# Residual stream of a two-layer trunk kept token-major: output projections with moving weights, norms along rows, modulation as rows

## The chip, the cores and the metric

The kernel runs on one core of a Trainium2 chip. The metric is the device time of one execution in microseconds (us). The engines are PE (TensorE, matrix products and transposes), DVE (VectorE), ACT (ScalarE), POOL (GpSimd) and SP (SyncE, which here issues most of the transfers). PE keeps 128 rows of a stationary matrix and streams columns of a moving one past it; results land in PSUM, which has banks of 512 fp32 columns by 128 partitions.

## The reference

640 tokens (128 of a prompt, 512 of a sample) of width D = 1024 go through two layers. The prompt and the sample have different modulation vectors, so each of the six modulation rows of a layer exists twice.

```python
for layer in range(DEPTH):
    mod = (silu(cond) @ w_mod[layer] + b_mod[layer])[:, None, :]
    sh1, sc1, g1, sh2, sc2, g2 = split(mod, 6, axis=-1)
    h = _modulate(x, norm_mix_g[layer], sh1, sc1)
    y, st = mixer(h, ...)          # layer 0: attention + gated delta, layer 1: SSD; ends in  o @ w_out
    x = x + g1 * y
    h = _modulate(x, norm_mlp_g[layer], sh2, sc2)
    x = x + g2 * _sq_relu_mlp(h, w_mlp_in[layer], w_mlp_out[layer])
return _rms_norm(x, final_norm_g)

def _modulate(x, gain, shift, scale):
    return _rms_norm(x, gain) * (1 + scale) + shift
def _sq_relu_mlp(h, w_in, w_out):
    a = maximum(h @ w_in, 0)
    return (a * a) @ w_out
```

In layer 1 the mixer's output is itself normed over 2048 features before w_out.

## The kernel before

**Layout.** The residual stream is feature-major: `xt` has 128 partitions of features, 8 blocks of features (KT), 640 tokens in the free dimension. All large products are made of three: each operand is split into a high part of a shorter type and a low part that is what is left, and hi x hi, lo x hi and hi x lo are added in PSUM. `wload` (L251) brings 1 MB of weights (`wraw`) by SP, `wpart` (L258) makes `whi` on ACT (L263) and `wlo` on DVE (L266).

**Products.** `gemm` (L273) makes one output tile: 128 output features (stationary weights) by 320 tokens (moving, half of the 640, HU), 8 blocks of features x 3 products = 24 products (`gps`, L287). `stage` (L291) goes over blocks of 256 output features, both halves of the tokens, two tiles each. For the second MLP product the 4096 hidden features come in four blocks b of 1024; `residual` (L513) adds each block's result, times the gate, to `xt` in one DVE operation per token class (L517).

**Norms.** The sum over features runs across partitions, so it is made on PE: `token_r` (L430) squares on ACT (L446), adds with a matrix of ones into four groups of 32 PSUM partitions (`stps`, L448), turns the sums into a column (`stc`, L456), takes the reciprocal root on DVE (L225 to L230), and spreads it over partitions again (`rbps`, L466). `pins` and `NPIN` hold these small products between fixed numbers of products of the last `gemm`s. `modulate` (L473) then makes `hh` and `hl`, the split input of the next stage, per block of features.

**Modulation.** `mod_steps` (L316) makes 512 of the 6144 outputs of `silu(cond) @ w_mod` per chunk c, in two half steps of 4 blocks k. Six chunks of layer 0 run in `delta_in`, between the inputs of the delta heads, with one small product per k, split into four of 128 columns that go to four groups of 32 PSUM partitions (L331). The other 14 chunks run in the first MLP with the sums over k on DVE (L352) and ACT and a short product at the end (`macc`, `msel`). `mod_out` (L306) turns the result into columns.

**Stages in time**: first norm and attention inputs (to 100 us), delta inputs with modulation (100 to 235), attention and delta heads (to 505), output projection `oute` with the norm ahead of the MLP (508 to 590), first MLP (to 1062, with the norm ahead of layer 1), SSD mixer (to 1553), output projection `outo` with its norm (to 1702), second MLP and `final` (L1584).

The order on each engine is set by a scheduler at build time from the order in the code and from when buffers come free; `issue_after` fixes single places.

Of the kernel before, what the change touches and what calls it, by code (L numbers as in the profile page):

```python
# [11 lines left out]
F32 = mybir.dt.float32  # L12
# [27 lines left out]

NPIN = (16, 8, 30, 24)
# [20 lines left out]
def _stream(i):  # L62
# [28 lines left out]
    for c in range(4):  # L91
        put(("oute", c), _cols(i["w_out_even"][0], c * 256, c * 256 + 256))
# [6 lines left out]
    for c in range(4):  # L99
        for kh in range(2):  # L100
            put(("outo", c, kh), _cols(i["w_out_odd"][0][kh * D:(kh + 1) * D], c * 256, c * 256 + 256))
    for layer in range(2):
        for b in range(4):
            for c in range(4):
                c0 = b * D + c * 256
                put(("m1", layer, b, c), _cols(i["w_mlp_in"][layer], c0, c0 + 256))
            for c in range(4):
                put(("m2", layer, b, c), _cols(i["w_mlp_out"][layer, b * D:(b + 1) * D], c * 256, c * 256 + 256))
# [3 lines left out]
def _params(i):  # L112
# [18 lines left out]
    put(("bmod", 1), _fm(i["b_mod"][1]))  # L131
    put(("gmix", 1), _fm(i["norm_mix_g"][1]))
    for layer in range(2):
        put(("gmlp", layer), _fm(i["norm_mlp_g"][layer]))
    put("gfin", _fm(i["final_norm_g"]))
# [57 lines left out]
class Prog:  # L193
    def __init__(self, nc, tc, ctx, io, widx, pidx, cidx, csmall, taps=None):
        self.nc, self.tc, self.ctx, self.io = nc, tc, ctx, io
        self.turn, self.share = 0, False
        self.sqb = 2
        self.behind = None
        self.mlast = None
        self.pins = []  # L200
        self.widx, self.pidx, self.cidx, self.csmall = widx, pidx, cidx, csmall
# [66 lines left out]

    def wblock(self, key, n=256):
        raw = self.wload(key, n)  # L270
        return [self.wpart(raw, c, min(P, n - c)) for c in range(0, n, P)]

    def gemm(self, w, xs, hf, half, m=P, cols=None):  # L273
# [6 lines left out]
        todo = [(k, q) for k in range(n) for q in range(3)]  # L280
        while todo:
            pin, m = self.pins.pop(0) if self.pins else (None, len(todo))
            if m > len(todo):
                self.pins.insert(0, (pin, m - len(todo)))
            with self.tc.issue_after(pin.ins) if pin else nullcontext():
                for k, q in todo[:m]:
                    self.nc.tensor.matmul(ps, ws[k // KT][q // 2][:, k % KT, :], xs[q % 2][k][:, c], start=k == 0 and q == 0, stop=k == n - 1 and q == 2)  # L287
            todo = todo[m:]
        return ps

    def stage(self, keys, xs, half, evac, tail=None, side=None):  # L291

        for i in range(0, len(keys), 2):
# [5 lines left out]
            for hf in range(2):  # L299
                for j, w in enumerate(tiles):  # L300
                    evac(2 * i + j, hf, self.gemm(w, xs, hf, half))
                if tail and i + 2 >= len(keys):
                    tail(hf)


    def mod_out(self, layer, m, ps):  # L306

        nc = self.nc
        n = ps.shape[1] // 32
        t = self.small.tile([P, P], F32, name="modt", tag="modt")[:, :32 * n]  # L310
        nc.vector.transpose(out=t, in_=ps)
        nc.vector.tensor_tensor(
            out=self.mod[layer][:, m:m + n, :], in0=t.rearrange("p (m c) -> p m c", c=32)[:, :, 0:2],
            in1=self.par(("bmod", layer))[:, m:m + n].rearrange("p (m o) -> p m o", o=1).to_broadcast([P, n, 2]), op=ALU.add)

    def mod_steps(self, todo, landing, pool=None, after=None):  # L316
# [11 lines left out]
        def product(lhs, x, start, stop):  # L328
            x = x.rearrange("p (m c) -> p m c", c=P)
            for q in range(4):  # L330
                nc.tensor.matmul(ps[32 * q:32 * q + 32], lhs, x[:, :, 32 * q:32 * q + 32], start=start, stop=stop)  # L331

        for i in range(n + 1):
            if i < n:
# [4 lines left out]
                raws.append(raw.rearrange("p (k c) -> p k c", c=512))  # L339
            if i:  # L340
                layer, c = todo[(i - 1) // 2]
                if i % 2:
                    ps = self.pmod.tile([P, 512], F32, name="modps", tag="mod")[:, :P]
# [1295 lines left out]
```

## Time and profile before

| | us |
|---|---|
| median of 3 runs | 2166.95 (2163.21 to 2169.73) |
| the profiled execution | 2170.79 |
| its span, first to last instruction | 2168.8 |
| PE busy | 2085.4 |
| DVE busy | 1353.2 |
| ACT busy | 908.3 |
| POOL busy | 158.5 |

The span is what the trace covers; the execution's own time is 2 us longer. Busy time is a sum over the whole span, so it says which engine is full on average, and not in which stage another one is waited for. Two products that follow each other overlap, so a product's duration is longer than its distance to the next; costs on PE are read from starts.

### The profile page before, as it was taken

Reading aid. Unit: us, or ns where it says so; the run is one execution under the profiler, and the core shown is the slowest. Engines: PE = TensorE matmul, PEld = TensorE weight load, DVE = VectorE, ACT = ScalarE, POOL = GpSimd, SP = SyncE. Lnnn points to the kernel's source line nnn. Section 1 sums busy time; section 2 is a strip of 40 time slices with the busy share of each in tenths; the row PEclk is TensorE's granted clock in tenths of the full one; section 3 lists DMA queues with packets and bytes.
Section 4 is the critical chain, followed back from the end, with each engine's and each line's share of the span. In section 5 each row is a group of like instructions: output and inputs, shape, how many; then the busy total and the mean of one; then the engine's idle time right before and its main releaser. Section 6 shows DMA issues by size and latency. Waiting matters only on the chain.

```text
span 2168.8 us, 36690 instructions
## 1 busy us (share of the span) xinstructions
PE 2085.4 (96%) x15045; PEld 1974.3 (91%) x15045; DVE 1353.2 (62%) x2775; ACT 908.3 (42%) x1914; POOL 158.5 (7%) x114
## 2 busy tenths in 40 slices
PE   6999799899999999999999999999899999999997
PEld 5999687788899999999799999999899999999996
DVE  6386867755696767673679877777643734344343
ACT  4345445353342414232468676676511523222230
POOL 1041302100000000000000001111200000000000
PEclk9999899899999999999999999999999999999998
DMA  7251101004244434432134433333321122222111
GB/s 325 104 214 40 38 1 35 1 4 158 88 156 156 156 136 156 137 117 83 74 113 144 152 120 112 137 127 121 138 72 64 61 78 78 78 78 74 67 56 49
DMA packets 53464, 222.09 MB, mean 102 GB/s; under 512 B 6282, under 2 KB 22642, under 8 KB 32434
## 3 DMA queue, kind: packets, MB, share of 16 engines
q1 hardware_dynamic: 43136, 205.26, 26.7%
q10 hardware_dynamic: 10162, 14.50, 1.9%
q8 instruction: 118, 1.93, 0.4%
q14 instruction: 48, 0.39, 0.1%
HBM read 211.40 MB, written 8.34 MB: 101 GB/s over the span
## 4 chain that ended last, share of the span: by engine, by line
PE 87%; DVE 6%; ACT 3%; DMA 3%; issue 1%; SPq 0%; POOL 0%; ACTq 0%; DVEq 0%; POOLq 0%
PE gps L287 67%; PE atps L625 2%; PE avps L1182 2%; PE yps L1534 2%; PE stps L448 1%; DMA bc<-afs 1%; PE offps L1548 1%; PE scps L1124 1%; PE dps L883 1%; PE stps L1565 1%; ACT bc L1519 1%; PE modps L331 1%; DVE wlo L266 1%; DMA wraw<-wall 1%; PE dps L889 1%
## 5 line engine op out<-in xcount | busy, mean ns | idle before, releaser
L287 PE MATMUL gps<-hh,whi 128*128 128x322 f32 (+3 forms) x1552 | 489.9, 316 | 1.6 <-ACT whi L263 1.1
L287 PE MATMUL gps<-hl,whi 128*128 128x322 f32 (+3 forms) x1552 | 485.4, 313 | 0.3 <-DVE hl L505 0.3
L287 PE MATMUL gps<-hh,wlo 128*128 128x322 f32 (+3 forms) x1552 | 484.4, 312 | 0.3 <-DVE wlo L266 0.3
L263 ACT CAST whi<-wraw 128x1024 fp32r<-128x1024 f32 (+2 forms) x220 | 231.7, 1056 | 534.0 <-PE gps L287 492.5
L287 PE MATMUL gps<-hidh,whi 128*128 128x320 f32 x1024 | 317.4, 310 | 0.0
L287 PE MATMUL gps<-hidl,whi 128*128 128x320 f32 x1024 | 316.1, 309 | 0.0
L287 PE MATMUL gps<-hidh,wlo 128*128 128x320 f32 x1024 | 315.8, 308 | 0.0
L266 DVE TENSOR_TENSOR wlo<-wraw,whi 128x1024 fp32r<-128x1024 f32 (+1 forms) x209 | 260.9, 1250 | 81.5 <-ACT whi L263 81.1
L287 PE MATMUL gps<-yh,whi 128*128 128x320 f32 x1280 | 304.7, 310 | 1.1 <-ACT yh L1262 1.1
L287 PEld LDWEIGHTS gps<-hh,whi 128*128 128x128 f32 (+1 forms) x1552 | 291.9, 188 | 9.0 <-issue 5.7
L287 PEld LDWEIGHTS gps<-hl,whi 128*128 128x128 f32 (+1 forms) x1552 | 291.7, 188 | 5.3 <-issue 3.2
L287 PEld LDWEIGHTS gps<-hh,wlo 128*128 128x128 f32 (+1 forms) x1552 | 292.1, 188 | 1.9 <-issue 1.1
L287 PE MATMUL gps<-yh,wlo 128*128 128x320 f32 x768 | 238.0, 310 | 0.0
L517 DVE SCALAR_TENSOR_TENSOR xt<-gps,mod,xt 128x128 f32<-128x128 f32 (+1 forms) x216 | 88.0, 437 | 227.4 <-PE gps L287 227.2
L287 PEld LDWEIGHTS gps<-yh,whi 128*128 128x128 f32 x1280 | 220.2, 189 | 2.9 <-ACT yh L1262 1.2
L287 PEld LDWEIGHTS gps<-hidh,whi 128*128 128x128 f32 x1024 | 192.1, 188 | 2.8 <-issue 1.6
L287 PEld LDWEIGHTS gps<-hidl,whi 128*128 128x128 f32 x1024 | 192.1, 188 | 1.0 <-issue 1.0
L287 PEld LDWEIGHTS gps<-hidh,wlo 128*128 128x128 f32 x1024 | 192.1, 188 | 0.0
L287 PEld LDWEIGHTS gps<-yh,wlo 128*128 128x128 f32 x768 | 145.2, 189 | 0.1
L352 DVE SCALAR_TENSOR_TENSOR macc<-wraw,condst,macc 128x512 f32<-128x512 f32 x196 | 137.2, 747 | 1.2 <-ACT macc L355 1.2
L530 DVE TENSOR_SCALAR hr<-gps 128x320 f32<-128x320 f32 x128 | 62.9, 491 | 109.4 <-PE gps L287 109.3
L531 ACT ACTIVATE hr<-hr 128x320 f32<-128x320 f32 x128 | 60.1, 469 | 152.3 <-DVE hr L530 152.2
(398 smaller groups left out, 3282.3 us busy)
## 6 DMA issues: line engine op xcount, KB each, us to landing
wraw<-wall SPq DMA_DIRECT2D x158, 1024.0 KB, 4.9
bc<-afs SPq DMA_DIRECT2D x40, 512.0 KB, 3.8
Q<-afr SPq DMA_DIRECT2D x64, 128.0 KB, 3.2
xt<-xt ACTq DMA_DIRECT2D x2, 2560.0 KB, 11.7
X<-growd SPq DMA_DIRECT2D x8, 320.0 KB, 6.1
xd<-xt ACTq DMA_DIRECT2D x1, 2560.0 KB, 8.6
xt<-xd SPq DMA_DIRECT2D x1, 2560.0 KB, 10.0
S<-ss ACTq DMA_DIRECT2D x16, 128.0 KB, 2.3
```

Of the source, the lines that this page charges most:

```text
L263: self.nc.scalar.copy(out=hi, in_=raw[:, :, c:c + m])
L266: eng.tensor_tensor(out=lo, in0=raw[:, :, c:c + m], in1=hi.bitcast(F32), op=ALU.subtract)
L287: self.nc.tensor.matmul(ps, ws[k // KT][q // 2][:, k % KT, :], xs[q % 2][k][:, c], start=k == 0 and q == 0, stop=k == n - 1 and q == 2)
L331: nc.tensor.matmul(ps[32 * q:32 * q + 32], lhs, x[:, :, 32 * q:32 * q + 32], start=start, stop=stop)
L352: nc.vector.scalar_tensor_tensor(out=a, in0=x, scalar=w, in1=a, op0=ALU.mult, op1=ALU.add)
L448: pin = nc.tensor.matmul(ps[r:r + 32, :HU], self.ones32, sq, start=k < 4, stop=k >= nk - 4)
L517: self.nc.vector.scalar_tensor_tensor(out=x[:, dst], in0=ps[:, src], scalar=gate[:, m, q:q + 1], in1=x[:, dst], op0=ALU.mult, op1=ALU.add)
L530: nc.vector.tensor_scalar(out=r, in0=ps, scalar1=0.0, scalar2=None, op0=ALU.max)
L531: nc.scalar.activation(out=r, in_=r, func=AF.Square)
L625: nc.tensor.matmul(ps[:, :n], x[k][:, TOFF[t]:TOFF[t] + P], w[:, k, :], start=k == 0 and q == 0, stop=k == KT - 1 and q == 2)
L1182: nc.tensor.matmul(acc, val(c, i), p, start=c == 1, stop=c == 6)
L1534: nc.tensor.matmul(py[q * 64:q * 64 + 64, pr * P:(pr + 1) * P], X[t](1 + d)[:, hh * 64:hh * 64 + 64], D[t][:, d, hh, :], start=d == 0, sto ...
```

## The change

The residual stream becomes token-major: `x` has 128 tokens of a tile in the partitions, 5 tiles (NT), 1024 features in the free dimension. Output projections and second MLP products (`by_rows`) take the activations as the stationary operand (128 tokens) and stream 512 columns of weights; five PSUM banks, one per token tile, are filled side by side, first for output features 0 to 511 (hm=0), then for the rest (hm=1). In a stage with a norm behind it, the last 8 blocks of hm=1 are held back and run tile by tile. `gated` adds a bank to `x` in two DVE operations. Norms are sums along rows, on ACT with an accumulator; `modulated` scales on DVE with rows of shift and scale, and PE transposes each tile back to features (`hps`), from which ACT and DVE make the split input. Modulation results stay rows: one product of 512 columns, two rows of bias and gain added, and written to DRAM (`modr`), from where `bands` spreads them over the partitions.

```diff
+    def by_rows(self, keys, parts, evac, done=None, side=None, pre=()):
...
+        def products(ps, t, k, w, j):
+            c = slice(t * P, (t + 1) * P)
+            for q, (x, y) in enumerate(((0, 0), (0, 1), (1, 0))):
+                nc.tensor.matmul(ps, parts[x][k][:, c], w[y][:, j, :], start=k == 0 and q == 0, stop=k == n - 1 and q == 2)
+
+        for hm in range(2):
+            banks, held = [], []
+            for i, key in enumerate(keys(hm)):
+                raw = None if pre else self.wload(key, 256)
...
+                for j in range(2):
+                    w = pre.pop(0) if raw is None else self.wpair(raw, j)
+                    k = 4 * i + 2 * j
+                    if done and hm and k >= n - KT:
+                        held.append((k, w))
+                        continue
+                    banks = banks or [self.pg.tile([P, 512], F32, name="rps", tag="g") for _ in range(NT)]
+                    for kk in range(2):
+                        for t in range(NT):
+                            products(banks[t], t, k + kk, w, kk)
+            for t in range(NT):
+                ps = banks[t] if banks else self.pg.tile([P, 512], F32, name="rps", tag="g")
+                for k, w in held:
+                    for kk in range(2):
+                        products(ps, t, k + kk, w, kk)
+                evac(t, hm, ps)
+                if done and hm:
+                    done(t)
+
+    def gated(self, t, hm, ps, gate, r=None):
...
+            v.tensor_tensor(out=ps, in0=ps, in1=g, op=ALU.mult)
...
+        v.tensor_tensor(out=self.x[:, t, c], in0=self.x[:, t, c], in1=ps, op=ALU.add)
...
+        def square(t, hm, junk):
+            nc.scalar.activation(out=junk, in_=self.x[:, t, hm * 512:hm * 512 + 512], func=AF.Square, scale=D ** -0.5, accum_out=ss[:, t, hm:hm + 1])
...
+        def scaled(t, r):
+            q = min(t, 1)
+            for j in range(2):
+                y = halves(t, j)
+                c = slice(j * 512, j * 512 + 512)
+                v.scalar_tensor_tensor(out=y, in0=self.x[:, t, c], scalar=r[:, t:t + 1], in1=scale[:, q, c], op0=ALU.mult, op1=ALU.mult)
+                v.tensor_tensor(out=y, in0=y, in1=shift[:, q, c], op=ALU.add)
+                todo.append((t, 4 * j, y))
+
+        def turned(t, a, y):
+            ps = self.pn.tile([P, 512], F32, name="hps", tag="n")
+            for k in range(4):
+                nc.tensor.transpose(ps[:, k * P:(k + 1) * P], y[:, k * P:(k + 1) * P], self.ident)
...
+            self.mlast = nc.scalar.copy(out=hi, in_=ps)
+            v.tensor_tensor(out=lo, in0=ps, in1=hi.bitcast(F32), op=ALU.subtract)
+
+        def done(t):
+            if t in (2, 3):
+                while todo:
+                    turned(*todo.pop(0))
+            if t in (1, 2, 4):
+                a = 2 if t == 2 else t - 1
+                r = root(a, t + 1)
+                for u in range(a, t + 1):
+                    scaled(u, r)
+            if t == 4:
+                while todo:
+                    turned(*todo.pop(0))
...
         def product(lhs, x, start, stop):
-            x = x.rearrange("p (m c) -> p m c", c=P)
-            for q in range(4):
-                nc.tensor.matmul(ps[32 * q:32 * q + 32], lhs, x[:, :, 32 * q:32 * q + 32], start=start, stop=stop)
+            nc.tensor.matmul(ps, lhs, x, start=start, stop=stop)
...
-        np_, self.pn, self.pg = self.pools(e1, ("mn0", 1, "left"), ("pn1", 4, None), ("pg2", 4, None))
...
-        self.stage([("oute", c) for c in range(4)], (hh, hl), HU, lambda m, hf, ps: self.residual(m, hf, ps, gate), half)
+        np_, self.pn, self.pg = self.pools(e1, ("mn0", 1, "left"), ("pn1", 2, None), ("pg2", 6, None))
...
+        self.by_rows(lambda hm: [("oute", hm, kq) for kq in range(2)], (hh, hl), evac, done)
...
-            rb = [self.token_r(rp, [ysq] + sq, 2 * D, hf, False) for hf in range(2)]
...
+            self.by_rows(lambda hm: [("outo", hm, kq) for kq in range(4)], (hh, hl), evac, done, pre=pre)
...
+            def done(t):
+                r = root(t, t + 1)
+                for j in range(2):
+                    c = slice(j * 512, j * 512 + 512)
+                    y = self.x[:, t, c]
+                    nc.vector.scalar_tensor_tensor(out=y, in0=y, scalar=r[:, t:t + 1], in1=gf[:, c], op0=ALU.mult, op1=ALU.mult)
+                    (nc.scalar, nc.sync)[j].dma_start(out=self.io["o_y"][:, t, c], in_=y)
```

Left out of the diff: the weights of oute, outo and m2 are stored in another order for `by_rows`, `wpair` splits 2 blocks of 512 columns as `wpart` split 8 of 128, and `pins`, `NPIN`, `residual` and `final` are gone. POOL no longer makes `wlo` at outo.

How the order changes on PE in `delta_in`, where `gps` are the inputs of the delta heads and `modps` the modulation products. Before:

```order
L287 MATMUL gps<-hh,whi 128x322
L287 MATMUL gps<-hl,whi 128x322
L287 MATMUL gps<-hh,wlo 128x322
L331 MATMUL modps<-wraw,condst 32x128 x16
L287 MATMUL gps<-hh,whi 128x322
L287 MATMUL gps<-hl,whi 128x322
```

After, in the same place:

```order
L304 MATMUL gps<-hh,wlo 128x322
L304 MATMUL gps<-hh,whi 128x322
L462 MATMUL modps<-wraw,condst 32x512 x4
L304 MATMUL gps<-hl,whi 128x322
L304 MATMUL gps<-hh,wlo 128x322
```

The half step stands where it stood; 16 products of 128 columns are now 4 of 512.

On PE between outo and the second MLP. Before, the last of the norm's small products (`rbps`) stand among the products of outo's last tile (`yh` is outo's input):

```order
L287 MATMUL gps<-yh,wlo 128x320
L287 MATMUL gps<-yh,whi 128x320 x2
L287 MATMUL gps<-yh,wlo 128x320
L466 MATMUL rbps<-con,rr 128x128 x2
L466 MATMUL rbps<-con,rr 128x64
L287 MATMUL gps<-yh,whi 128x320 x2
L287 MATMUL gps<-yh,wlo 128x320
```

After, `rps` are outo's banks, `hps` the transposes (8 per token tile), and `gps` the first products of the MLP (their input is stored in the buffers of `yh`):

```order
L330 MATMUL rps<-wlo,yh_15023 128x512
L330 MATMUL rps<-whi,yl 128x512
L409 MATMUL hps<-con,hrow 128x128 x32
L304 MATMUL gps<-yh_15022,whi 128x320
L304 MATMUL gps<-yh_15023,whi 128x320
```

The transposes of the last four tiles stand between the last product of outo and the first of the MLP, with no product among them.

On DVE in the second MLP, where one block b of the second product goes over from hm=0 to hm=1. Before, `xt<-gps` is `residual`, `wlo` the split of weights:

```order
L517 SCALAR_TENSOR_TENSOR xt<-gps,mod_70,xt 128x192
L517 SCALAR_TENSOR_TENSOR xt<-gps,mod_70,xt 128x320
L266 TENSOR_TENSOR wlo<-wraw,whi 128x1024
L517 SCALAR_TENSOR_TENSOR xt<-gps,mod_70,xt 128x320
L266 TENSOR_TENSOR wlo<-wraw,whi 128x1024
```

After, the five banks' gating (L363 in PSUM, L366 into `x`):

```order
L363 TENSOR_TENSOR rps<-rps,gate 128x512 x2
L366 TENSOR_TENSOR x<-x,rps 128x512
L363 TENSOR_TENSOR rps<-rps,gate 128x512
L366 TENSOR_TENSOR x<-x,rps 128x512
L363 TENSOR_TENSOR rps<-rps,gate 128x512 x2
L366 TENSOR_TENSOR x<-x,rps 128x512
L279 TENSOR_TENSOR wlo<-wraw,whi 128x1024
L366 TENSOR_TENSOR x<-x,rps 128x512 x2
L279 TENSOR_TENSOR wlo<-wraw,whi 128x1024 x3
```

One fused operation per tile became two per bank, the five banks come in a row, and a split of weights stands ahead of the last two banks' additions.

## Rows read from the trace of the kernel before

**Rows 1.** The page: PE's busy us (share of the span), instructions.

```profile
PE 2085.4 (96%) x15045; PEld 1974.3 (91%) x15045; DVE 1353.2 (62%) x2775; ACT 908.3 (42%) x1914; POOL 158.5 (7%) x114
```

**Rows 2.** Stretches A:B: length; busy PE, PEld, DVE, ACT, POOL; PEclk, DMA share, GB/s.

```profile
100.00:235.00 135.00, 130.45 (x1188) 124.84 (x1187) 98.94 (x210) 67.19 (x196) 39.98 (x32) 0.99 0.35 127
...
670.00:988.00 318.00, 318.00 (x2287) 313.75 (x2285) 225.88 (x391) 100.16 (x160) 0.00 (x0) 1.00 0.40 139
...
1702.00:2126.00 424.00, 424.00 (x2892) 424.00 (x2893) 173.60 (x289) 121.38 (x193) 0.00 (x0) 1.00 0.20 70
```

**Rows 3.** The chain that ended last: start us, length us, work.

```profile
698.49 28.36 PE gps L287 x192
```

**Rows 4.** Timeline of PE, delta_in and first MLP: start us, us, engine, line, operation.

```profile
118.14 1.96 PE L331 MATMUL modps<-wraw,condst 128*32 128x128 f32 x64
120.03 0.42 PE L287 MATMUL gps<-hl,whi 128*128 128x322 f32 x1
...
697.84 0.64 PE L331 MATMUL modps<-macc,msel 128*32 128x128 f32 x16
698.42 0.41 PE L287 MATMUL gps<-hh,whi 128*128 128x320 f32 x1
```

**Rows 5.** Timeline of PE, attention (512 columns) and SSD (transposes).

```profile
495.73 0.39 PE L1155 MATMUL scps<-qm,kst 128*128 128x512 f32 x1
495.96 1.02 PE L1182 MATMUL avps<-pp,vc 128*128 128x512 f32 x2
496.82 0.61 PE L1190 MATMUL scps<-con,au 128*128 128x1 f32 x5
...
1177.12 0.77 PE L1384 MATMUL xkps<-con,so 128*128 128x128 f32 x5
1177.72 0.60 PE L1565 MATMUL stps<-xa,xk 128*128 128x256 f32 x2
```

**Rows 6.** Stretches of the four norms, L287 on PE alone: length, busy (products), PEclk.

```profile
554.70:589.60 34.90, 23.95 (x151) 1.00 0.31 121
1029.50:1062.00 32.50, 21.95 (x137) 1.00 0.26 101
1666.10:1701.60 35.50, 23.95 (x151) 1.00 0.17 60
2130.50:2150.80 20.30, 14.99 (x98) 1.00 0.19 65
```

**Rows 7.** DVE by line and form: count, busy us, mean ns, idle before.

```profile
L266 DVE TENSOR_TENSOR wlo<-wraw,whi 128x1024 fp32r<-128x1024 f32 x206 | 255.5, 1242 | 79.5 <-ACT whi L263 79.1
L352 DVE SCALAR_TENSOR_TENSOR macc<-wraw,condst,macc 128x512 f32<-128x512 f32 x196 | 137.2, 747 | 1.2 <-ACT macc L355 1.2
...
L1549 DVE TENSOR_TENSOR Q<-Q,offps 128x512 f32<-128x512 f32 x32 | 21.7, 685 | 15.8 <-PE offps L1548 13.7 <-ACT Q L1544 1.9
```

**Rows 8.** Timeline of DVE: 512 columns in SBUF; an rsqrt, 11 operations, first and last.

```profile
1534.62 0.69 DVE L1551 TENSOR_TENSOR Q<-Q 128x512 f32<-128x512 f32 x1
...
2157.42 0.17 DVE L225 TENSOR_SCALAR rsi<-ms 128x3 int32<-128x3 int32 x1
...
2159.39 0.16 DVE L230 SCALAR_TENSOR_TENSOR rr<-rsa,rr 128x3 f32<-128x3 f32 x1
```

**Rows 9.** ACT by line and form, 512 columns from PSUM.

```profile
L1385 ACT COPY xk<-xkps 128x512 f32<-128x512 f32 x24 | 13.9, 580 | 8.2 <-PE xkps L1384 8.1
```

**Rows 10.** Timeline of PE: starts of oute and outo, the wait before in brackets.

```profile
508.16 0.56 PE L287 MATMUL gps<-op,whi 128*128 128x320 f32 x2 [2.92 <-ACT whi L263]
...
1560.51 0.64 PE L287 MATMUL gps<-yl,whi 128*128 128x320 f32 x1 [5.94 <-DVE yl L1263]
```

**Rows 11.** The first stretch of outo on PE: length, busy (products), PEclk.

```profile
1556.90:1563.70 6.80, 3.19 (x12) 0.50 1.02 405
```

**Rows 12.** Timeline of PE: the last product.

```profile
2150.80 0.31 PE L287 MATMUL gps<-hidh,wlo 128*128 128x320 f32 x1
```

**Rows 13.** The chain that ended last: its last piece.

```profile
2163.17 2.77 DVE xt L1590 x6
```

More of the change, by code (lines that the diff above doesn't have):

```diff
@@ L98, in _stream @@
         put(("sz", g), _cols(w, g * 256, g * 256 + 256))
[L99 to L101 removed]
+    rowblocks(("outo",), i["w_out_odd"][0])
     for layer in range(2):
@@ L279, in gemm, with stage @@
         n = len(ws) * KT
[L280 to L288, printed above, removed]
+        for k in range(n):
+            for q in range(3):
+                self.nc.tensor.matmul(ps, ws[k // KT][q // 2][:, k % KT, :], xs[q % 2][k][:, c], start=k == 0 and q == 0, stop=k == n - 1 and q == 2)
         return ps
-    def stage(self, keys, xs, half, evac, tail=None, side=None):
+    def stage(self, keys, xs, half, evac, side=None):
         for i in range(0, len(keys), 2):
@@ L320, in mod_steps @@
+    def mod_steps(self, todo, landing, small, pool=None, after=None):
         nc = self.nc
@@ L535, in mlp @@
             self.stage([("m1", layer, b, c) for c in range(4)], xs, HU, act, side=side)
-            self.stage([("m2", layer, b, c) for c in range(4)], (hh, hl), HU,
-                       lambda m, hf, ps: self.residual(m, hf, ps, gate), tail if b == 3 else None, side)
+            if b == 0:
+                g = self.bands(evac[0].tile([P, 2, D], F32, name="gate"), layer, 5)
+                gate = [g[:, :, c:c + 512] for c in (0, 512)]
+            if b == 3 and late:
+                done = late()
+            self.by_rows(lambda hm: [("m2", layer, b, hm, kq) for kq in range(2)], (hh, hl),
+                         lambda t, hm, ps: evac[1](t, hm, ps, gate[hm], b == 3), done if b == 3 else None, side)
     def conv_silu(self, pool, out, w, xs, cw, bias, pre=None):
@@ new lines, in odd @@
+            for t in range(NT):
+                for j, y in enumerate([ysq] + sq):
+                    nc.tensor.matmul(pc[:, t:t + 1], y[:, t * P:(t + 1) * P], self.cst("stat"), start=j == 0, stop=j == 2)
+            ym, yr = (np_.tile([P, NT], F32, name=n, tag=n) for n in ("ym", "yr"))
+            nc.vector.tensor_scalar(out=ym, in0=pc[:, :NT], scalar1=16.0 / D, scalar2=EPS, op0=ALU.mult, op1=ALU.add)
+            self.rsqrt(np_, yr, ym, [P, NT])
+            self.x = xp.tile([P, NT, D], F32, name="x")
@@ new lines, in odd, with evac @@
+            nc.sync.dma_start(out=self.x, in_=self.xd)
+            gate = self.bands(np_.tile([P, 2, 512], F32, name="gate"), 1, 2, 0)
+            shift, scale = (self.bands(np_.tile([P, 2, D], F32, name=f"band{kind}"), 1, kind) for kind in (3, 4))
+            square, done = self.modulated(np_, scale, shift, h, [P * t for t in range(NT)],
+                                          lambda t, j: np_.tile([P, 512], F32, name="hrow", tag="hrow", bufs=4))
+            def evac(t, hm, ps):
+                self.gated(t, hm, ps, gate, yr)
+                square(t, hm, ps)
+                if t == NT - 1 and hm == 0:
+                    self.bands(gate, 1, 2, 1)
```

318 lines of the change are left out of this document (177 added, 141 removed).

## The prediction

> **What bounds the kernel now.** I read the engines' shares first: PE is busy 96% of the span [rows 1]; no other engine is past 62%. An average hides stages, so the next view is the table by stage [rows 2]. From 670 to 988 us (first MLP) and from 1702 to 2126 us (second MLP) PE is busy for the whole stretch; from 100 to 235 us (inputs of the delta heads, with the modulation products among them) it is busy 130.45 of 135 us, so at most 4.5 us there can absorb anything. The chain of waits says the same: its longest pieces are products of L287 back to back [rows 3], 192 of them in 28.36 us, 0.1477 us each. So PE time added in these stages is added to the end, PE time saved is saved, and DVE matters only where PE waits for it: at the norms (called T1 after oute, T2 after the first MLP, T3 after outo, and the final one) and at the start of a stage.
>
> **A. Modulation products in delta_in.** Before, one half step is 16 products of 128 columns, four at a time in four groups of 32 PSUM partitions. The trace shows two such half steps in a row: 118.14 to 120.03 us [rows 4], 1.89 us for 64 records, 8 k; with the 16 records, 2 k, in 0.58 us from 697.84 to 698.42 that is (1.89 - 0.58) / 6 = 0.22 us per k and 0.14 for the switch. After, each k is one f32 product of 512 columns. What that takes is read from the attention's f32 products [rows 5]: two records from 495.96 to 496.82, which are one 128x512 product (an f32 product of 512 columns stands as two records), 0.86 us. The new one has 32 output rows instead of 128, but the same 512 columns pass, so I take 0.86. Difference 0.64 us per k, 12 half steps of 4 k: 12 x 4 x 0.64 = 31. Of PE's 4.5 us of idle time some 4 can take it up: **+27** (24 to 31).
> The four groups of the old form start nearly together: 64 records in 1.89 us is 0.03 us per record, although each has 128 columns. The Trainium skill, "TensorE: Matmul & The Clock Gate", section "Why this matters for your kernels", advises just that for small outputs: put them at PSUM partitions 32j so that each lands in its own column group, and they run at once. It speaks against this edit, and the trace agrees.
>
> **B. The pooled modulation products in the first MLP.** The sums over k are made on DVE and ACT as before; only the product at the end changes, from 16 records, 0.44 us without the switch [rows 4], to 2 products of 0.86. 14 chunks x (1.72 - 0.44) = **+18**, on a PE that is 100% busy there [rows 2].
>
> **C. The three norms between stages.** Before: in the stretch of a norm I count the L287 products, take 0.1477 us for each, and call the rest the norm's price on PE [rows 6]: T1 34.9 - 151 x 0.1477 = 12.6; T2 32.5 - 137 x 0.1477 = 12.3; T3 35.5 - 151 x 0.1477 = 13.2; 38 in all. After, the statistics are gone from PE, but each norm has 40 transposes; five of them took 0.60 us [rows 5], 0.12 each, 4.8 us per norm. The larger part is DVE's. In the last half of a stage that a norm follows, PE runs tile by tile: 24 products x 0.232 = 5.6 us per tile of 128 tokens. DVE has per tile: the gating in two operations (685 ns from PSUM [rows 7], 0.69 us in SBUF [rows 8]), scale and shift for two halves (4 x 0.70 = 2.8), two lo parts from PSUM (1.4), together 5.6, and three times per norm an rsqrt of 12 small operations 0.2 us apart [rows 8], 2.3 us, or 1.4 per tile: 7.0 us against 5.6. So DVE falls behind by 1.4 us per tile, 7 in all. And tiles 3 and 4 are scaled only when tile 4's sum of squares is there: gating 1.4, Square on ACT 0.6 to 0.8 (a 128x512 pass takes 580 ns [rows 9]), rsqrt 2.3, two tiles x 2.9 = 5.8, the last transpose, copy and lo 2.3. With the 40 transposes' 4.8: 7 + 1.4 + 0.8 + 2.3 + 5.8 + 2.3 + 4.8 = 24. In T3 PE's order has nothing to run meanwhile: all 32 remaining transposes stand ahead of the first product of the MLP. T2 has a few products between, too few to matter. In T1 38 and 27 products of the MLP (5.6 and 4.0 us) stand between, some 8 to 9 us of cover: 16. So T1 +3, T2 +12, T3 +11. A wait of that length also costs clock: after the 5.94 us wait at 1560.51 the granted clock was 0.50 (the 1.2 of the two levels 1.2 and 2.4 GHz) and 12 products took 3.19 us instead of 1.77 [rows 10, 11]; PE was idle for the rest of that stretch. For two or three such restarts with somewhat more products each I take +6. Sum **+32**; 15 if DVE keeps pace until the last tile, 45 if the fill and rsqrt lie one after the other everywhere.
>
> **D. PSUM hand-over.** by_rows holds five banks of 512 columns at once out of six. PE finishes them 3 x 0.232 = 0.70 us apart, and starts the other half (hm=1) at once in the sixth and then in those that DVE has emptied. DVE needs 1.38 us per bank (two operations where residual had one), and the order puts a weight split (1242 ns [rows 7]) ahead of the fourth bank's second operation. Bank 3 is free 5 x 0.685 + 4 x 0.69 + 1.24 = 7.4 us after bank 0 was full; PE wants it after 5 x 0.70 + 3 x 0.70 = 5.6. The wait is 1.8 to 2.2 us, three times in layer 1 and once in outo; in layer 0 the pooled sums (747 ns each [rows 7]) stand between as well, 3.5 us each, three times. 4 x 2.1 + 3 x 3.5 = **+18**. No row of before shows such a hand-over, since there one output tile took 24 products (3.5 us) and DVE one or two operations: the ends are 0 (the splits all run ahead) and 25.
>
> **E. The products themselves.** 4224 of 320 columns become 2640 of 512, the same number of columns. 4224 x 0.1477 = 624. For 512 columns in the split type the row at 495.73 starts the next one at 495.96 [rows 5], 0.23; I take 0.232: 612, **-11**. Ends: 0.225 by the row's rounding, and 0.236 by the price per column of [rows 3] (0.1477 / 320): -30 to 0.
>
> **F. The end.** Before, the last product starts at 2150.80 and the span ends at 2168.8 [rows 12], and with the statistics between the products the final norm costs 38.3 - 98 x 0.1477 = 24 [rows 6]. After, tile 4's end is gating 1.4, Square 0.8, rsqrt 2.3, two operations 1.4, and the last transfer 2.9 as now (the last DVE operation ends at 2165.94 [rows 13]), with 1 for a DVE that is a little behind: 10. **-14** (-16 to -10).
>
> **G. Starts of oute and outo.** There PE waits 2.92 us for a weight cast, and 5.94 for DVE's yl [rows 10]. by_rows takes k outside, so 15 products (3.5 us) follow each pair of input parts, and the norm's factor is applied per token afterwards, without its statistics ahead of the first bank. **-6** (-12 to 0).
> Gate, shift and scale rows now come by DMA from DRAM, queued on SP with the weights; they are issued a stage ahead, so I cost them at nothing; were one late, the hand-over would wait about as long as a transfer takes, 2.9 us by the one in F.
>
> **Sum**: 27 + 18 + 32 + 18 - 11 - 14 - 6 = +64 on the profiled 2170.79 us: 2235. That execution lies 3.8 above the median of the runs, so 2231.
>
> **Rivals.**
> R1, faster: DVE keeps up. If per tile it needs less than PE's 5.6 us (rsqrt in waiting time, its operations shorter), and splits stand ahead of the hand-over, then a norm costs its transposes and one short fill, about 5 us (15 instead of 38, -23), and D is 0. 27 + 18 - 23 - 11 - 14 - 6 = -9: 2158. For it: DVE was only 62% busy. Against it: the per-tile sum of 7.0 is from rows, and the order holds tiles 3 and 4 together. 7%.
> R2, width pays: a fixed part per product, which 512 columns spread over more work. At the low end of E: -30 instead of -11, 2212. Against it: 147.7 ns for 320 columns and 230 for 512 are 0.46 and 0.45 ns per column, with next to nothing fixed in it. 12%.
> The same page of the Trainium skill, section "Back-to-back issue gap", gives N / 2.4 + 2.5 ns for a product of N columns, 215.7 ns for 512; by that E would be -54 and the time about 2188. The rows do not follow it: it would give 136 ns for 320 columns, where they show 147.7.
> R3, modulation is covered: in delta_in PE's added 0.64 pieces fill time in which it would have waited for DVE or transfers later, at half of A, and the norms at their low end: 64 - 14 - 17 = +33: 2200. Against it: 130.45 of 135 us busy. 13%.
> R4, DVE as the bound: hand-overs at 25 and norms at 45, with rows from DRAM once late: 64 + 7 + 13 + 3 = +87: 2254. 14%.
> R5, the change's parts cancel to nothing, E at -30 and C at 15 with D at 0: 64 - 19 - 17 - 18 = +10: 2177. 4%.
>
> **How the numbers follow.** My forecast has 50%. What a measurement of this kernel can tell from no change is about 0.3%, 6.5 us. Faster: R1, 7%. Within it: part of R1 and R5, 5%. Slower: the rest, 88%. The range reaches over R3, R2 and R4: 2188 to 2262.
>
> **What would show it.** In the profile after: products of L462 that start 0.86 us apart (A, B); idle time of PE ahead of hps and of the first product after it, ended by DVE, near 15 to 20 us in T2 and T3 (C); waits of rps 1.8 to 3.5 us long, ended by DVE's second gating operation, seven times (D); rps 0.23 apart (E); 10 us from the last rps to the end (F). The forecast is wrong if PE shows no idle time at the norms, or if L462's products take 0.22 each.

## The result and the profile after

The changed kernel takes 2229.99 us (median of 4 runs, 2222.48 to 2235.86) against 2166.93 before: ratio 1.029, 95% interval 1.0246 to 1.0334. Slower by 63 us, with 64 in the sum and 2231 forecast. The profiled execution is 2224.19 us, span 2222.4, so its stages add up to 53.6 more than before. Another execution of the same program (e0_after below) spent 281.7 us instead of 275.3 in one stage, the heads; the rest below repeats within 3 us.

The page after, busy us and share of the span:

```profile
PE 2112.9 (95%) x12883; PEld 1851.6 (83%) x12883; DVE 1386.5 (62%) x2606; ACT 897.9 (40%) x1892; POOL 151.1 (7%) x112
```

PE was 2085.4 [rows 1]: 27 us more busy time (products at the lower clock count with their longer duration), and the other 26 us of the span are waits of PE. The stages, worked out from the starts of PE's products in the two traces (kvps: last products of a delta head's input; avps: attention's values):

| stage | before | after | difference |
|---|---|---|---|
| start to first kvps | 122.64 | 139.12 | +16.5 |
| first to last kvps (rest of delta_in) | 111.12 | 125.91 | +14.8 |
| attention and delta heads, to the last avps | 265.28 | 275.26 | +10.0 |
| to oute's first product | 9.13 | 9.84 | +0.7 |
| oute, T1, first block's m1 | 131.40 | 133.16 | +1.8 |
| first MLP, from its first hidden operand to its last | 411.14 | 417.42 | +6.3 |
| T2 to the first SSD transpose | 31.79 | 46.67 | +14.9 |
| SSD, first to last of those transposes | 393.62 | 389.35 | -4.3 |
| end of SSD, to outo's first product | 77.61 | 83.46 | +5.9 |
| outo, T3, first block's m1 | 196.62 | 199.26 | +2.6 |
| second MLP, first hidden operand to last | 400.46 | 392.71 | -7.8 |
| last product to the end | 17.98 | 10.25 | -7.7 |

A and B as they look after: the chain (start, length, work) in delta_in, and PE's timeline around a pooled chunk in the first MLP.

```profile
102.55 3.55 PE modps L462 x8
```

```profile
697.04 0.40 PE L330 MATMUL rps<-whi,hidl 128*128 128x512 f32 x1
697.37 1.90 PE L462 MATMUL modps<-macc,msel 128*32 128x512 f32 x4
699.21 0.50 PE L330 MATMUL rps<-whi,hidh 128*128 128x512 f32 x1
```

Eight records are four products, one half step: 3.55 us, 0.89 each, where [rows 4] show 1.89 us for two half steps. The pooled chunk's two products hold PE from 697.37 to 699.21, 1.84 us, where they took 0.58.

The second MLP, from the chain: each block of m1 and of m2 is one uninterrupted piece.

```profile
1819.60 56.00 PE rps L330 x240
1875.61 56.31 PE gps L304 x384
```

240 products of 512 columns in 56.00 us are 0.2333 each; and there is no wait at the hand-over from hm=0 to hm=1, which falls at 1847.6 inside the first piece.

T3 on PE, all rows but the single products (start, length, operation, wait before in brackets):

```profile
1736.42 1.04 PE L409 MATMUL hps<-con,hrow 128*128 128x128 f32 x8
1739.63 1.03 PE L409 MATMUL hps<-con,hrow 128*128 128x128 f32 x8
1747.78 1.94 PE L409 MATMUL hps<-con,hrow 128*128 128x128 f32 x8 [7.12 <-DVE hrow L403]
1754.47 1.94 PE L409 MATMUL hps<-con,hrow 128*128 128x128 f32 x8 [4.75 <-DVE hrow L403]
1756.96 1.97 PE L409 MATMUL hps<-con,hrow 128*128 128x128 f32 x8 [0.55 <-DVE yh L413]
1760.32 0.90 PE L304 MATMUL gps<-yh,whi 128*128 128x320 f32 x2 [1.40 <-DVE yh L413]
```

Transposes of eight take 1.04 us at first and 1.94 after the 7.12 us wait: the granted clock is 0.50 there, the lower level. DVE in the same stretch:

```profile
1735.86 1.23 DVE L279 TENSOR_TENSOR wlo<-wraw,whi 128x1024 fp32r<-128x1024 f32 x1 [0.59 <-ACT whi L276]
...
1745.54 1.41 DVE L402 SCALAR_TENSOR_TENSOR hrow<-x,nr,band 128x512 f32<-128x512 f32 x2
...
1750.99 2.73 DVE L402 SCALAR_TENSOR_TENSOR hrow<-x,nr,band 128x512 f32<-128x512 f32 x4
1753.64 2.49 DVE L403 TENSOR_TENSOR hrow<-hrow,band 128x512 f32<-128x512 f32 x4
```

Tiles 3 and 4 are scaled together from 1750.99 to 1756.1, 5.1 us for the 5.8 of the prediction; splits of the MLP's weights (the first row and three more) stand on DVE in the same chain.

T2 on PE: one of the first and the last half tiles.

```profile
1104.49 1.09 PE L409 MATMUL hps<-con,hrow 128*128 128x128 f32 x4 [2.96 <-DVE hl L413]
...
1117.13 0.93 PE L409 MATMUL hps<-con,hrow 128*128 128x128 f32 x4
1119.51 0.61 PE L409 MATMUL hps<-con,hrow 128*128 128x128 f32 x4
1121.53 0.66 PE L409 MATMUL hps<-con,hrow 128*128 128x128 f32 x4 [1.40 <-DVE hl L413]
1123.59 0.66 PE L409 MATMUL hps<-con,hrow 128*128 128x128 f32 x4 [1.40 <-DVE hl L413]
```

The last ones are 2.06 us apart, and each waits for the low part of the one before: there is one PSUM buffer for the transposes (pool pn2), which the prediction did not look at.

The end, DVE's first and last rows after PE's last product, which starts at 2212.15:

```profile
2212.58 0.70 DVE L363 TENSOR_TENSOR rps<-rps,gate 128x512 f32<-128x512 f32 x1 [0.85 <-PE rps L330]
...
2217.94 1.42 DVE L1451 SCALAR_TENSOR_TENSOR x<-x,nr,gf 128x512 f32<-128x512 f32 x2
```

From 2212.15 to 2222.4 are 10.25 us; [rows 12, 13] had 18.0, and some 6 us of statistics between the products ahead of that.

### The profile page after: what moved, and what is told of

It reads as the page before. It is cut to its first block, busy times and chain, and to the rows that moved or that the text cites. A ratio compares the mean times of both kernels' runs of the same rounds, so it can differ in the third digit from the quotient of the medians.

```text
span 2222.4 us, 32146 instructions
## 1 busy us (share of the span) xinstructions
PE 2112.9 (95%) x12883; PEld 1851.6 (83%) x12883; DVE 1386.5 (62%) x2606; ACT 897.9 (40%) x1892; POOL 151.1 (7%) x112
## 4 chain that ended last, share of the span: by engine, by line
PE 90%; DVE 5%; DMA 2%; ACT 2%; issue 1%; POOL 0%; SPq 0%; DVEq 0%; ACTq 0%; POOLq 0%
PE gps L304 42%; PE rps L330 28%; PE modps L462 3%; PE yps L1695 2%; PE atps L749 2%; PE avps L1326 2%; PE offps L1709 1%; PE stps L1726 1%; DMA X<-growd 1%; PE scps L1268 1%; DMA wraw<-wall 1%; PE dps L1027 1%; PE dps L1033 1%; PE xkps L1545 1%; PE hps L409 1%
## 5 line engine op out<-in xcount | busy, mean ns | idle before, releaser
L304 PEld LDWEIGHTS gps<-hh,whi 128*128 128x128 f32 (+1 forms) x1552 | 293.5, 189 | 18.4 <-issue 7.6
L330 PE MATMUL rps<-wlo,hidh 128*128 128x512 f32 x640 | 253.0, 395 | 0.0
L330 PE MATMUL rps<-whi,hidh 128*128 128x512 f32 x640 | 252.3, 396 | 0.0
L330 PE MATMUL rps<-whi,hidl 128*128 128x512 f32 x640 | 251.5, 395 | 0.0
L276 ACT CAST whi<-wraw 128x1024 fp32r<-128x1024 f32 (+2 forms) x132 | 140.0, 1062 | 259.0 <-PE rps L330 178.9
L288 DVE TENSOR_TENSOR wlo<-wraw,whi 128x1024 fp32r<-128x1024 f32 x88 | 108.9, 1240 | 189.8 <-ACT whi L287 189.7
L279 DVE TENSOR_TENSOR wlo<-wraw,whi 128x1024 fp32r<-128x1024 f32 (+3 forms) x123 | 156.8, 1276 | 106.4 <-ACT whi L276 105.7
L287 ACT CAST whi<-wraw 128x1024 fp32r<-128x1024 f32 x88 | 91.7, 1048 | 276.2 <-PE rps L330 199.3
L330 PEld LDWEIGHTS rps<-whi,hidh 128*128 128x128 f32 x640 | 120.2, 188 | 33.4 <-ACT macc L489 4.2
L330 PEld LDWEIGHTS rps<-whi,hidl 128*128 128x128 f32 x640 | 120.2, 188 | 29.0
L330 PEld LDWEIGHTS rps<-wlo,hidh 128*128 128x128 f32 x640 | 120.3, 188 | 28.5
```

Source lines behind the costliest of these rows:

```text
L276: self.nc.scalar.copy(out=hi, in_=raw[:, :, c:c + m])
L279: eng.tensor_tensor(out=lo, in0=raw[:, :, c:c + m], in1=hi.bitcast(F32), op=ALU.subtract)
L287: self.nc.scalar.copy(out=hi, in_=x)
L288: self.nc.vector.tensor_tensor(out=lo, in0=x, in1=hi.bitcast(F32), op=ALU.subtract)
L330: nc.tensor.matmul(ps, parts[x][k][:, c], w[y][:, j, :], start=k == 0 and q == 0, stop=k == n - 1 and q == 2)
```

## The experiments

The price of a norm below is always worked out as in the prediction's C: the time from the norm's first transpose to 60 PE records after its last, less 0.2333 for each rps and 0.1475 for each gps in it. In the changed kernel it is 14.3 (T1), 24.7 (T2) and 24.3 (T3). T3's price has a scatter of its own: in the changed kernel (twice), e1_groups, e2_pn2 and e6_gp each wait inside T3 is the same to 0.01 us, but the price goes from 21.4 to 24.3, because the clock comes back at different times. The first 5.6 us of the MLP behind T3 in the changed kernel and in e6_gp (length, busy PE and products, PEclk):

```profile
1760.40:1766.00 5.60, 5.60 (x21) 0.50 0.00 0
```

```profile
1701.30:1706.90 5.60, 5.60 (x39) 1.00 0.01 3
```

The first 60 products take 11.45 us there and 8.75 here. So a difference of T3 under 3 us is read from its waits, not from its price.

**The changed kernel again.**

> The changed kernel once more, to see how far its parts repeat: 2222 to 2236 us as in the runs shown. If the 10 us that the delta and attention heads lost (265 to 275 us between the last kvps and the last avps) belong to the order of the program, they are here again; if they belong to one execution, the heads take 265 to 270 here.

Measured: 2231.14 us (2221.39 to 2238.76), 1.0285 [1.025, 1.0319]. All stages but the heads repeat within 2.5 us; the heads took 281.73 us. So their loss is not one execution's accident, and it varies by 6 us.

**Modulation products in four groups again.**

```diff
-            nc.tensor.matmul(ps, lhs, x, start=start, stop=stop)
+            for q in range(4):
+                nc.tensor.matmul(ps[32 * q:32 * q + 32], lhs, x[:, q * P:(q + 1) * P], start=start, stop=stop)
```

(bias and gain rows are stored in the four groups' layout, and four transfers of 128 columns write a chunk to DRAM.)

> The changed kernel with its modulation products again in four groups of 32 PSUM partitions, 128 columns each; rows as before. Theory (the wide product leaves three of four groups idle and its time lies on PE's path): delta_in gives back 48 x 0.66 = 31 us and the first MLP 14 x 1.25 = 17, so 49 less than the changed kernel on the same chip, 2174 to 2186, where the heads may move by 10 either way with the order. Rival (the added time in delta_in filled waits that come anyway): only the 17 of the MLP and at most half of the 31, above 2197.

Measured: 2168.62 us, 1.0002 [0.9992, 1.0011] of the kernel before, so 62 us less than the changed kernel: the slowdown is gone, more than the 49 expected and below the 2174 to 2186. A half step in its PE timeline:

```profile
101.19 1.08 PE L465 MATMUL modps<-wraw,condst 128*32 128x128 f32 x32
102.20 0.42 PE L304 MATMUL gps<-hh,whi 128*128 128x322 f32 x1
```

1.01 us instead of 3.55. By stages against the changed kernel's profile: the two stages up to the last kvps -27.5, the first MLP's two stages -18.4, the heads -13.4. The first two are A and B; the rival falls. The heads are the part beyond the 49. (With the layout DVE's bias and gain operations on a chunk shrink too, from 512 columns to 128; PE's own rows, 3.55 against 1.01 us, account for A without that.)

**The wide product's cost in the kernel before.** In delta_in alone, a product of 384 columns per k beside the four of 128:

```diff
+            if not pool:
+                nc.tensor.matmul(wide, lhs, x[:, :384], start=start, stop=stop)
```

> The kernel before with one more product of 384 columns per k beside the four of 128 in delta_in alone (its result is not used): the cost of the wide product by itself, 384 columns x 4 passes = 0.64 us. The order in the heads stays that of before. Theory: 48 x 0.64 = 31 more than before, 2198, and the heads take 265 us as before. Rival (cover in delta_in): under 2182. If the heads take 275 us here too, the time in delta_in, not the order, is what slows them.

Measured: 2195.04 us, 1.0121 [1.0105, 1.0136]: 27 us more. Its PE timeline, the same record of two neighbouring k (the four products of 128 stand between):

```profile
118.20 0.49 PE L330 MATMUL modwide<-wraw,condst 128*32 128x384 f32 x1
...
119.06 0.49 PE L330 MATMUL modwide<-wraw,condst 128*32 128x384 f32 x1
```

0.86 us per k, as the wide product of 512 in the changed kernel. On PE that is 48 x 0.64 = 31, and 27 reach the end: the prediction let delta_in's idle time absorb 4, and PE, busy for 130.45 of the 135 us from 100 to 235 in [rows 2], is busy for all 135.00 here. The heads took 267.4 us, with the order of before and a delta_in that ends at 260.6 us (265.0 in the changed kernel, 233.8 before); so a later delta_in by itself slows them by 2 us at most.

**A second PSUM buffer for T2's transposes.**

```diff
-                ("pn2", 1, None), ("pmod2", 1, None), ("pg3", 6, None))
+                ("pn2", 2, None), ("pmod2", 1, None), ("pg3", 5, None))
```

> The changed kernel with two PSUM buffers for the transposes ahead of layer 1 (one before) and five instead of six banks for products in the first MLP. Theory: after the last tiles are scaled, transpose, copy and low part follow each other through one buffer, 2.06 us per half tile, and two buffers overlap them: T2 falls by 3 to 5 us; five banks cost nothing, since PE's order works the free bank ahead. Rival 1 (DVE alone sets T2): no change, within 1 us. Rival 2 (the hand-over of banks does cost): the second products of the first MLP get longer by 1 to 2 us at each of the three hand-overs.

Measured: 2216.99 us, 1.0237 [1.0204, 1.027]; 14 less than the changed kernel by the medians; the stage of T2 takes 38.51 us instead of 46.67, its price is 16.9 instead of 24.7. These 8 us are more than the 3 to 5 expected (the rest of the 14 is not in T2; the heads alone vary by 6): the one buffer also held up the transposes of the earlier tiles (the first row of T2 above). T2's last transposes on PE:

```profile
1115.35 1.23 PE L409 MATMUL hps<-con,hrow 128*128 128x128 f32 x8 [1.06 <-DVE hrow L403]
1117.66 1.25 PE L409 MATMUL hps<-con,hrow 128*128 128x128 f32 x8 [1.09 <-DVE hl L413]
```

Eight at a time, 2.3 us apart, instead of four 2.06 apart. The first MLP takes 418.16 us with five banks and 417.42 with six, so the sixth bank is worth 0.7 us in all three hand-overs.

**Both together.**

> The changed kernel with the modulation products in four groups (e1_groups) and the second transpose buffer ahead of layer 1 (e2_pn2) together. If the two costs are separate, their gains add: 62 and 14 by the medians, 62 and 8 by the stages; about 2158 to 2160, faster than the kernel before by 7 to 9 us. If e2_pn2's gain only moved a wait, 2165 to 2169.

Measured: 2163.0 us, 0.9977 [0.9965, 0.9989]: faster than before by 5 us. Against e1_groups 5.6 by the medians and 7.6 by T2's stage (39.11 from 46.69); the two costs are separate. T1, T2, T3: 14.1, 17.5, 21.5.

**T3's order.** On e6_gp, the transposes of tiles 3 and 4 are issued behind the first half of the MLP's first block:

```diff
                 for j, w in enumerate(tiles):
                     evac(2 * i + j, hf, self.gemm(w, xs, hf, half))
+                if mid:
+                    mid()
+                    mid = None
...
-            if t == 4:
-                while todo:
-                    turned(*todo.pop(0))
+            if t == 4 and not late:
+                rest()
```

> e6_gp, and in T3 the transposes of token tiles 3 and 4 stand behind the first 96 products of the second MLP instead of ahead of them (their rows are kept in a pool that stays open). Theory of the prediction (T3 costs PE some 22 us because its order has nothing to run while DVE scales tiles 3 and 4): 96 x 0.147 = 14 us of products move into the wait, 8 to 14 us less than e6_gp, and no half clock after it. Rival (DVE is the bound there: the MLP's own DVE work and weight splits only push tiles 3 and 4 later): within 3 us of e6_gp, the wait then stands before the second half.

Measured: 2154.48 us, 0.9936 [0.9917, 0.9955], 8.5 less than e6_gp (7.4 by the stage of outo and T3) and the fastest of all kernels here. T3's price falls from 21.5 to 14.8. T3 on PE, its transposes, and the piece of the chain between them:

```profile
1683.18 1.94 PE L412 MATMUL hps<-con,hrow 128*128 128x128 f32 x8 [7.12 <-DVE hrow L406]
...
1699.72 1.03 PE L412 MATMUL hps<-con,hrow 128*128 128x128 f32 x8
```

```profile
1685.12 14.77 PE gps L304 x96
```

The wait of 7.12 us for the scaled tile 2 is still there; the later one, 4.75 in e6_gp as in the changed kernel, is filled by 96 products, and the transposes behind them run at 1.03 us per eight, not at 1.94. The theory holds: what stood behind T3 was the order of PE, for the part behind tile 2.

**A root per tile.** On e6_gp, `if t in (1, 2, 4)` becomes one root for each of tiles 2, 3 and 4.

> e6_gp with a reciprocal root per tile for tiles 2, 3 and 4 instead of one for 3 and 4 together: tile 3 is scaled before tile 4's sum is there, for one more rsqrt of 2.2 us per norm. Theory (the tail of tiles 3 and 4 on DVE, 5.8 us, is the wait): T1, T2 and T3 shorten by 2 to 3 us each, 6 to 9 in all. Rival (DVE's total work over the tiles is the wait): each gets longer by 1 to 2 us.

Measured: 2171.43 us, 1.002 [1.0011, 1.0029], 8.4 more than e6_gp. Prices 13.7, 19.4, 24.7: T2 is 1.9 us longer, T3 3.2, of which 1.4 are the clock's later return (the first 60 products behind it take 10.16 us instead of 8.75). T3 on PE:

```profile
1693.44 1.94 PE L409 MATMUL hps<-con,hrow 128*128 128x128 f32 x8 [7.22 <-DVE hrow L403]
1698.87 1.94 PE L409 MATMUL hps<-con,hrow 128*128 128x128 f32 x8 [3.49 <-DVE hrow L403]
1704.24 1.94 PE L409 MATMUL hps<-con,hrow 128*128 128x128 f32 x8 [3.43 <-DVE hrow L403]
```

Tile 3's transposes come 1.2 us earlier than in e6_gp (16.9 us after the first ones, there 18.1), but tile 4's 1.7 us later (22.3 and 20.5), and the MLP's products stand behind both: DVE's total over the tiles is the bound, not the tail of two tiles. Some 4.5 us of the loss are in the first MLP, where PE waits once at a hand-over, with pooled sums among the gating on DVE, and then runs eight products at the lower clock, 0.43 us apart:

```profile
675.40 0.50 PE L330 MATMUL rps<-whi,hidh 128*128 128x512 f32 x1 [2.56 <-DVE x L366]
```

That is the wait of the prediction's D; a built order can bring it about, but the changed kernel's did not.

**Weight splits on POOL.** On e6_gp, every second of the first eight splits of each MLP.

```diff
+            self.share = b == 0
             self.stage([("m1", layer, b, c) for c in range(4)], xs, HU, act, side=side)
+            self.share = False
```

> e6_gp with every second weight split of the first 8 of each MLP on POOL instead of DVE. In the trace four splits of 1.22 us stand on DVE in the middle of T3's chain, and three in T1's. Theory (each on DVE delays the tiles by its time): two of four go, T3 and T1 shorten by 2 to 3 us each. Rival (POOL's splits take longer, 2.9 us each in the kernel before, and slow DVE in SBUF): no gain or up to 3 us more.

Measured: 2165.66 us, 0.9992 [0.9981, 1.0002], 2.7 more than e6_gp. T3's price is 24.5 instead of 21.5, T1's the same. Of T3's 3 us 1.4 are again the clock's return; from its first transpose to its last it takes 23.6 us instead of 22.1. POOL in T3, and a split that stayed on DVE:

```profile
1675.78 2.39 POOL L279 TENSOR_TENSOR wlo<-wraw,whi 128x1024 fp32r<-128x1024 f32 x1 [98.82 <-DVE nr L243]
1679.74 2.35 POOL L279 TENSOR_TENSOR wlo<-wraw,whi 128x1024 fp32r<-128x1024 f32 x1 [1.57 <-ACT whi L276]
```

```profile
1677.16 2.09 DVE L279 TENSOR_TENSOR wlo<-wraw,whi 128x1024 fp32r<-128x1024 f32 x1 [1.26 <-ACT whi L276]
```

2.4 us on POOL for 1.23 on DVE; two splits left DVE's chain, and T3 did not get shorter. The split on DVE that overlaps with POOL's first takes 2.09 us; the 190 of this kernel that overlap with no operation of POOL take 1.23 at most. That is 0.9 us of what DVE was to gain, lost beside POOL's work, as the rival had it. What the rest comes from, the order of DVE among it, was not separated.

**Three operations per bank.** In the changed kernel's second MLP, one more DVE operation ahead of the gating:

```diff
+                if not last:
+                    nc.vector.tensor_tensor(out=ps, in0=ps, in1=gf[:, 0:512], op=ALU.mult)
                 self.gated(t, hm, ps, gate)
```

> The changed kernel with one more DVE operation of 128x512 per PSUM bank, ahead of the gating, in blocks 0 to 2 of the second MLP's second product (the output's values are changed by it). Theory of the prediction (PE takes the banks of hm=1 in turn and waits for the fourth): three operations per bank free bank 3 some 9 to 10 us after bank 0 is full, PE wants it after 5.6, so 3 to 4 us more at each of three hand-overs, 402 to 405 us from the first to the last product of the second MLP instead of 392.7. Rival (the built order gives the free sixth bank 17 to 24 products at once, which covers the hand-over): 392.7 again, within 0.5.

Measured in a single run: 392.70 us from the first to the last product of the second MLP, as in the changed kernel (392.71), and the chain has the same pieces:

```profile
1817.95 56.00 PE rps L330 x240
```

The prediction's theory of D falls. The built order shows why: with the banks' numbers, the products of a block's hm=1 do not go round the five banks from the start. In the changed kernel the first bank gets 17 of its 24 products at once, then the second 5, and so on; here the first gets all 24. That is 4.0 and 5.6 us of work in the one bank that is free. The order is made anew for each kernel, so this run does not show what a third operation would cost under the changed kernel's order; it shows that neither kernel waits.

**Without the shift.** On e6_gp, the addition of the shift rows is left out of the three norms, two operations per tile.

> e6_gp without the addition of the shift rows in the three norms (that part of the computation is left out): two DVE operations of 0.6 to 0.69 us less per token tile. Theory (DVE's work per tile sets the norms): tiles 3 and 4 alone are 2.5 us shorter, with the backlog of the tiles before 3 to 6 us less at each of T1, T2 and T3, where e6_gp has 14.1, 17.5 and 21.5 over its products. Rival (the chain of transpose, copy and low part through PSUM sets them): under 1 us each.

Measured: 2154.77 us, 0.9933 [0.9916, 0.995], 8.2 less than e6_gp. Prices 9.9, 13.4 and 19.7 for 14.1, 17.5 and 21.5: -4.2, -4.1 and -1.8. T3's price gains less than the 3 us at the lower end, but there the clock comes back later: the first 60 products behind T3 take 11.23 us instead of 8.75. From T3's first transpose to the MLP's first product, less the products between, it is 17.2 us instead of 21.5, -4.3. So DVE's work per tile sets all three norms, as expected. The transposes of tile 3 still wait:

```profile
1684.31 1.94 PE L408 MATMUL hps<-con,hrow 128*128 128x128 f32 x8 [4.99 <-DVE hrow L402]
```

**What stays open: the heads.** Their 10 to 16 us appear with the wide product in the token-major kernel, and are gone without it (261.9, where the kernel before has 265.3). The first 20 us after the last kvps, before, after, and in e5_before_wide (columns: length, busy PE, PEld, DVE, ACT, POOL, PEclk, DMA share, GB/s):

```profile
233.80:253.80 20.00, 11.93 (x52) 9.16 (x50) 19.76 (x40) 4.38 (x14) 10.62 (x9) 0.67 0.18 40
```

```profile
265.10:285.10 20.00, 6.55 (x30) 5.99 (x28) 18.90 (x36) 7.85 (x23) 16.27 (x13) 0.50 0.14 40
```

```profile
260.60:280.60 20.00, 10.66 (x47) 7.71 (x46) 19.61 (x38) 5.28 (x15) 11.73 (x10) 0.78 0.20 40
```

DVE is full in all three; after the change PE is busy for little more than half as long in this stretch, POOL more, and the clock is at its lower level. The built PE order of the heads is the same in before and in e5_before_wide (265.3 and 267.4 us); the changed kernel (275.3 and 281.7), e2_pn2 (277.4) and e10_gate3 (276.5) have another, and e1_groups, e6_gp and the kernels made from it a third (261 to 263). So the time goes with the order, and by e5_before_wide the wide product's time alone costs them 2 us at most. The order is the likely cause, not a shown one: a kernel with that order and the old products was not tried.

## Why the prediction was right, and where its steps were wrong

The forecast held to 1 us, and that is luck: 18 us (D) and 7 (C) too many cancelled against 10 to 16 for the heads, which were not in the sum, and smaller ones in A, E and G. The mechanisms of A, B and F were right, and that of C in the main.

- **A** (+27): right. The wide product is worth 27.5 us up to the last kvps by e1_groups, and 27 at the end in the kernel before. Up to the last kvps the changed kernel has 31.3 more; the other 4 are there in e1_groups too, and its heads give them back.
- **B** (+18): right. 1.84 for 0.58 us, 14 times, 17.6; e1_groups gave 18.4 back in the first MLP's stages. R3, modulation covered by other waits, is excluded by both.
- **C** (+32): right that DVE's work per tile sets the norms (e11_noshift), and that PE's order has nothing to run meanwhile (e9_t3); not right term by term. T1 14.3 for 16, T2 24.7 and T3 24.3 for 24, and 6 for the clock: 63.3 for 70, so +25 over the 38 of before. T2's number had a second cause, the one PSUM buffer, worth 8 us, which the list of waits did not contain; with two buffers T2 is 16.9. The waits were sized too long: in T3 the lower clock alone costs some 5 us (three times eight transposes at 1.94 us instead of 1.04, and 11.45 us instead of 8.75 for 60 products), which leaves 19 for the 24. One reason is in the rows: the sum takes 0.69 to 0.70 us for a DVE operation, and operations that follow each other start 0.60 to 0.66 apart. And that tiles 3 and 4 wait together for one root is not the bound (e7_root).
- **D** (+18): wrong, 0. The failed step is "starts the other half (hm=1) at once in the sixth and then in those that DVE has emptied", three products per bank in turn: that is the order of the code, not of the built program, which gives the free bank 17 of its products first. Of the 2640 rps in the trace none waits more than 0.1 us for anything, apart from the first of oute and of outo; the forecast had seven hand-overs with waits. The order was read by names without the buffers' numbers, which hide it. DVE's half of the step was nearly right: the fourth bank's addition starts 6.0 us after the first gating and the sum had it end after 7.4. R1 had D at 0 for another reason, splits ahead of the hand-over. (4 x 2.1 + 3 x 3.5 is 18.9, written as 18.)
- **E** (-11): 4224 products at 0.147 are 621.6 (0.1477 in layer 0, 0.1467 in layer 1), 2640 at 0.2333 are 616: -6, inside its bounds. R2, a fixed part that wide products save, is excluded: 0.456 ns per column at 512, 0.46 at 320.
- **F** (-14): right. 10.25 for 10, where before 18.0 and some 6 of statistics stood.
- **G** (-6): -2; neither start gained what was forecast. From the last avps to oute's 200th product, less the products, it is 11.7 us instead of 12.4; from the last SSD transpose to outo's 200th, 84.2 instead of 85.4 (82.5 in e0_after). At outo the first product waits longer than any in [rows 10], and starts at the lower clock again. On PE and on DVE:

```profile
1620.18 0.80 PE L330 MATMUL rps<-whi,yh 128*128 128x512 f32 x1 [7.39 <-ACT yh L1403]
```

```profile
1610.47 1.22 DVE L288 TENSOR_TENSOR wlo<-wraw,whi 128x1024 fp32r<-128x1024 f32 x1
...
1615.47 1.22 DVE L288 TENSOR_TENSOR wlo<-wraw,whi 128x1024 fp32r<-128x1024 f32 x1
1616.61 0.49 DVE L1530 SCALAR_TENSOR_TENSOR yt<-sz,yt 128x128 f32<-128x128 f32 x2
```

Four splits of weights, which POOL shared before, stand among the last SSD operations that outo's input comes from. The statistics left the path as forecast, and these came onto it; that they ate the gain is read from the order, no run took them away.
- **Not in the sum**: the heads, +10 to +16. The prediction took for granted that stages which the diff does not touch keep their time; their built order changed.

The parts are 31 + 18 + 25 + 0 - 6 - 14 - 2 = +52; with 10 to 16 for the heads that is 62 to 68, where the medians have 63 and the profiled execution 54. Of the 8 us or more between the parts and the profile, 4 are in SSD, whose length scatters (393.6 before, 390.0 in e5_before_wide, which leaves SSD as it was); the others lie in the seams of the stages and were not followed.

## What to carry to other kernels

A product with few output rows (32 here) that is made in four column groups at once took 0.22 us per k where one wide product takes 0.86 to 0.89, and on a PE that is nearly full the difference reaches the end (27 of 31 us in delta_in, 18 of 18 in the first MLP): turning it into one wide product cost more than all else in this change saved. Where DVE has more per tile than PE, look which products PE's order has to run meanwhile; moving 96 of them ahead of the last transposes gave 8.5 us, a second PSUM buffer 6 to 8. Before pricing a hand-over of buffers, read the built order with the buffers' numbers.

## What the runs showed of the hardware

- DVE operations of 128x512 that follow each other start 0.60 us apart, though each lasts 0.68 to 0.69 (DVE timeline of the changed kernel at the hand-over):

```profile
1846.15 0.68 DVE L366 TENSOR_TENSOR x<-x,rps 128x512 f32<-128x512 f32 x1
1846.74 0.69 DVE L363 TENSOR_TENSOR rps<-rps,gate 128x512 f32<-128x512 f32 x1
1847.35 0.68 DVE L366 TENSOR_TENSOR x<-x,rps 128x512 f32<-128x512 f32 x1
```

- One f32 product of 512 columns with 32 output rows takes 0.89 us, no less than one with 128 rows [rows 5].
- The same split of weights takes 2.4 us on POOL where DVE takes 1.23; and one on DVE took 2.09 us that overlapped with one on POOL (e8_pool).
- The same waits of PE can cost 3 us more or less: behind T3, with all its waits the same to 0.01 us, the granted clock was 1.00 at the MLP's first product in e6_gp and 0.50 for 6 us more in the changed kernel.
